# Experts' gate and up products in four column groups of 32 tokens, with the output summed in PSUM

## The chip, the core and the metric

The kernel runs on one core of one Trainium2 chip. The metric is the device time of one execution in microseconds; the time given for a kernel is the median of several runs. One more execution is recorded by the hardware profiler, and every row of a trace below comes from it.

## What is computed

The reference is a model of two blocks on 256 tokens of width 1024, all in float32. The first block has two layers of three mixers (attention, retention, mLSTM), the second one layer of attention and a linear recurrence, and then a mixture of experts. The change touches the experts alone:

```python
logits = (xf @ w_router + b_router).astype(jnp.float32)   # 256 x 32
top_v, top_i = lax.top_k(logits, TOP_K)                   # 4 of 32 experts a token
gates = jax.nn.softmax(top_v, axis=-1)
...
g = xb @ w_gate[e] + b_gate[e]          # 1024 x 1024
u = xb @ w_up[e] + b_up[e]              # 1024 x 1024
g = jnp.minimum(g, SWIGLU_LIMIT)
u = jnp.clip(u, -SWIGLU_LIMIT, SWIGLU_LIMIT)
glu = g * jax.nn.sigmoid(SWIGLU_ALPHA * g)
return ((u + 1.0) * glu) @ w_down[e] + b_down[e]   # 1024 x 1024
```

Each token's four outputs are weighted by its gates and added to x, and a last RMS norm follows. All 32 experts' weights are read, 12 MB an expert. How many tokens an expert gets follows from the reference and its fixed inputs; in order of the experts it is 63, 75, 47, 3, 55, 22, 47, 9, 57, 33, 21, 34, 13, 10, 24, 4, 19, 29, 20, 1, 13, 36, 39, 31, 22, 40, 35, 19, 22, 126, 27, 28. Two have more than 64 (experts 1 and 29), 13 have more than 32.

## The kernel before, in words

Everything runs in one program, written out by hand. The two blocks up to the router take the first 490 us or so. From there on `_build` goes through the 32 experts in a Python loop (L1304), so each expert's instructions stand once in the program.

Weights come in blocks of 128 x 2048 floats (1 MB), four each for gate, up and down, 12 an expert. They lie in slots of SBUF. `give` (L235) puts the next block in the order into a freed slot, on SyncE's queue; `release` (L247) gives a slot back when its last reader is through. SyncE issues strictly in order, so a transfer that waits for its slot holds all later ones. 19 blocks are under way or in place when the loop starts: expert 0's 12 and seven of expert 1.

A token that chose expert e has a rank in e's list. The kernel handles the first 64 ranks in the main path. `pick` (L1177) builds a one-hot of ranks, multiplies it with the normalised tokens (`xg`), copies the result and transposes it into xT, with the gain. `up` (L1228) calls `product` (L1215) for gate and for up: eight blocks of the contraction, each with two matmuls, one for output columns 0 to 511 into PSUM partitions 0 to 63, one for columns 512 to 1023 into partitions 64 to 127. So 64 tokens fill a column group of 64, and two column groups work on the two halves of the output. Every float32 matmul stands as two records in the trace (two passes). A bias matmul with K = 128 (`own`, which picks the expert's rows out of `bias`) is put into the product. `gated` (L1240) is a chain of five steps on VectorE and ScalarE. `down` (L1248) transposes the result, copies it to hT, and runs a third `product`. The output is copied to `ys`. After every second expert `place` (L1197) builds the matrix that brings outputs back to tokens, weighted with the gates, and `add` (L1262) multiplies with it and adds the result to x on VectorE, 8 matmul records for two experts. The down biases are added to x once, at expert 6 (`last_bias`, L1148).

Tokens beyond 64 go through blocks that are run on a condition, on every engine, nested for up to 256 tokens: `more_up` (L1276, its branch is recorded at L1278) repeats pick, gate, up and gating; `more_down` (L1283, recorded at L1284) repeats down, place and add. The eight gate and up slots are released after the first, the four down slots after the second. `foresee` (L1271) issues a hint for TensorE that a branch is likely taken, which means that the block is skipped; for `more_up` it stands after the gate product, for `more_down` after the first eighth of the down product or so.

Of the kernel before, what the change touches and what calls it, by code (L numbers as in the profile page):

```python
# [9 lines left out]
F32 = mybir.dt.float32  # L10
# [7 lines left out]
CAP = 64  # L18
# [8 lines left out]
def _col_layout():  # L27
    at, off = {}, 0
    for name, n in (
        ("norm0", 8), ("norm1", 8), ("y0", 4), ("y1", 4), ("cw0", 16), ("cw1", 16), ("cb0", 4), ("cb1", 4),  # L30
        ("n1g", 8), ("final", 8), ("cw2", 16), ("cb2", 4), ("ba", 8), ("bi", 8), ("lam", 8), ("og", 8), ("n2g", 8),
    ):
        at[name] = (off, n)
        off += n
    return at, off
# [9 lines left out]
def _constants():  # L45
# [38 lines left out]
    add("owner", np.where(p[:, None] // 64 == p[None, :] // 64, p[:, None] % 32, -1))  # L84
# [13 lines left out]
def _prep(i):  # L98
# [27 lines left out]
    b = np.stack([a["b_gate_2"][0], a["b_up_2"][0]], axis=1).reshape(32, 2, 2, 512).transpose(2, 0, 1, 3)  # L126
    z["bias"] = np.stack([b, b], axis=1).reshape(128, 1024)
    z["b_down"] = a["b_down_2"][0][:, :768].reshape(32, 3, 256).transpose(1, 0, 2).reshape(96, 256)
    z["b_down_end"] = a["b_down_2"][0][:, 768:].reshape(32, 2, 128).transpose(1, 0, 2).reshape(64, 128)
# [21 lines left out]
    put("n2g", a["norm2_g_2"][0])  # L151
    z["cols"] = c
# [43 lines left out]
def _build(tc, T, out):  # L196
# [577 lines left out]
    def mixer(xt):  # L774
# [242 lines left out]
        give(13, 15, 16, 17, 18, 21)  # L1017
# [15 lines left out]
        give(4, 5, 6, 7, 11)  # L1033
# [40 lines left out]
    ew = ctx.enter_context(tc.tile_pool(name="ew", bufs=1))  # L1074
    t22, t23 = slot(22), slot(23)
    xh = slot(12).rearrange("p (a b) -> p a b", a=2)
    bias = ew.tile([128, 1024], F32R, name="bias")
    xg, th = t22[:, 0:512], t22[:, 512:1024]
    more_h = [t22[:, 1024:1536], t22[:, 1536:2048], ew.tile([128, 512], F32, name="more")]
    ys, xTs = ([t23[:, o + 512 * k:o + 512 * k + 512] for k in range(2)] for o in (0, 1024))  # L1080
    nc.scalar.dma_start(rbc[0:96, :], T["b_down"])
    gates, rank = (sm(n, 2, 32, bufs=1) for n in ("gates", "rank"))
    count = small.tile([1, 32], I32, name="count", bufs=1)

    t14 = slot(14)

    def split_bias():

        b = t14[:, 256:1280]
        nc.scalar.dma_start(b, T["bias"])  # L1090
        S.activation(bias, b, AF.Copy)
        for p in (slice(32, 64), slice(96, 128)):
            V.tensor_tensor(bias[p], b[p], bias[p].bitcast(F32), op=OP.subtract)

    def router():
        xT = slot(10).rearrange("p (k t) -> p k t", k=8)
        wr, br = t14[:, 0:256], t14[:, 1536:1568]
        lg, mr = (t14[:, o:o + 72].rearrange("p (a b) -> p a b", a=2) for o in (1568, 1640))
        mask, m8, sel, nv = (t14[:, o:o + n].rearrange("p (a b) -> p a b", a=2)
                             for o, n in ((1712, 64), (1776, 16), (1792, 16), (1808, 4)))  # L1100
        nc.scalar.dma_start(wr, T["w_router"])
        load_row(br, "br")
        r, _ = x_stats(1e-5, xh, False, True)
        tt = [bank(n) for n in ("xg", "tr", "st", "y")]
# [10 lines left out]
        t = bank("g")  # L1115
        for hf in range(2):
# [3 lines left out]
            busy(ins, 8 if hf else 4, bank("cb", 2))  # L1120
# [15 lines left out]
        t = bank("u")  # L1136
# [5 lines left out]
        busy(ins, 4, bank("cb", 2))  # L1142
# [4 lines left out]

    def last_bias():  # L1148

        t = bank("tr")  # L1150
        gx = ew.tile([128, 2, 192], F32, name="hotw")[:, :, 0:96]
        V.tensor_copy(gx.rearrange("p a (q e) -> p a q e", q=3), gates[:, :, None, :].to_broadcast([128, 2, 3, 32]))
        for hf in range(2):
            PE.transpose(t[0:96, 128 * hf:128 * hf + 128], gx[:, hf, :], ident)
        V.tensor_copy(one[0:96, :], t[0:96, 0:256])
        for q, w, o in ((0, rbc, 0), (1, rbc, 256), (2, rbc, 512), (0, b_down, 768), (1, b_down, 896)):
            p, n = slice(32 * q, 32 * q + 32), w.shape[-1]
            t = bank("cb", 2)
            for hf in range(2):
                PE.matmul(t[:, n * hf:n * hf + n], one[p, 128 * hf:128 * hf + 128], w[p, :], start=True, stop=True)  # L1160
            d = x[:, :, o:o + n]
            V.tensor_tensor(d, d, two(t[:, 0:2 * n]), op=OP.add)

    router()
    b_down = before[0:64, :]
    nc.scalar.dma_start(b_down, T["b_down_end"])
    four = lambda v: v.rearrange("p (c s t) -> p c s t", c=4, s=2)
    gain = cols[:, COLS["n2g"][0]:COLS["n2g"][0] + 8].rearrange("p (s c) -> p c s", s=2)

    def ranks(e, j):  # L1170
        if not j:
            return rank[:, :, e]
        r = sm("rj", 2)
        V.tensor_scalar(r, rank[:, :, e], -64.0 * j, None, op0=OP.add)
        return r

    def pick(e, j):  # L1177

        r = ranks(e, j)
        one_hot = ew.tile([128, 2, 64], F32, name="hot", bufs=2)  # L1180
        for hf in range(2):
            V.tensor_scalar(one_hot[:, hf, :], slots[:, 0:64], r[:, hf:hf + 1], None, op0=OP.is_equal)  # L1182
# [5 lines left out]
        if e + j == 0:  # L1188
            busy(ins, 2, bank("cb", 2))
# [179 lines left out]
```

## Time and profile before

| what | us |
|---|---|
| median of 3 runs | 1562.95 (1562.74 to 1572.78) |
| the profiled execution | 1557.01 |
| its span, first to last instruction | 1555.1 |
| TensorE busy | 1406.8 |
| VectorE busy | 580.6 |
| ScalarE busy | 306.7 |

Busy time is what an engine's instructions cover, and matmuls that run side by side count once. Terms of the rows: PE is TensorE's matmuls, PEld its weight loads, DVE VectorE, ACT ScalarE, SP SyncE, and a q behind a name is that engine's sequencer, which issues transfers and takes branches. `out<-in` are the program's names (s is a slot; g, u, y, cb, tr, xg and st are PSUM banks), and x with a number is a count.

### The profile page before, as it was taken

Reading aid. Unit: us, or ns where it says so; the run is one execution under the profiler, and the core shown is the slowest. Engines: PE = TensorE matmul, PEld = TensorE weight load, DVE = VectorE, ACT = ScalarE, POOL = GpSimd, SP = SyncE. Lnnn points to the kernel's source line nnn. Section 1 sums busy time; section 2 is a strip of 40 time slices with the busy share of each in tenths; the row PEclk is TensorE's granted clock in tenths of the full one; section 3 lists DMA queues with packets and bytes.
Section 4 is the critical chain, followed back from the end, with each engine's and each line's share of the span. In section 5 each row is a group of like instructions: output and inputs, shape, how many; then the busy total and the mean of one; then the engine's idle time right before and its main releaser. Section 6 shows DMA issues by size and latency. Waiting matters only on the chain. (4 is left out here: it accounts for less than half of the span.)

```text
span 1555.1 us, 17575 instructions
## 1 busy us (share of the span) xinstructions
PE 1406.8 (90%) x6638; PEld 707.5 (45%) x6638; DVE 580.6 (37%) x1238; ACT 306.7 (20%) x551; POOL 170.8 (11%) x100
## 2 busy tenths in 40 slices
PE   7899989999879989999899999998999998999896
PEld 6687877888556333333333333333333333333332
DVE  4856467648786212222122212221222222222123
ACT  4335443454552000000000000000000000000001
POOL 3333333344240000000000000000000000000001
PEclk9899999999889999999999999999999999999998
DMA  8423443444258756999999999999999999999561
GB/s 296 160 91 127 137 163 109 142 148 139 81 196 337 297 210 264 419 417 370 412 401 420 407 416 408 377 419 418 417 418 410 419 419 406 413 420 419 235 252 63
DMA packets 67500, 469.31 MB, mean 302 GB/s; under 512 B 8128, under 2 KB 9440, under 8 KB 11744
## 3 DMA queue, kind: packets, MB, share of 16 engines
q1 hardware_dynamic: 65664, 463.38, 74.4%
q8 instruction: 142, 2.33, 0.6%
q10 hardware_dynamic: 1632, 3.10, 0.6%
q14 instruction: 62, 0.51, 0.1%
HBM read 465.40 MB, written 1.05 MB: 300 GB/s over the span
## 5 line engine op out<-in xcount | busy, mean ns | idle before, releaser
L1223 PE MATMUL g<-s,s 128*64 128x512 f32 x1088 | 289.4, 601 | 25.3 <-PEq L1284 23.4
L1223 PE MATMUL y<-s,hT 128*64 128x512 f32 x1088 | 256.5, 602 | 1.8 <-ACT hT L1253 1.8
L1223 PE MATMUL u<-s,s 128*64 128x512 f32 x1088 | 247.5, 596 | 0.0
L1223 PEld LDWEIGHTS g<-s,s 128*64 128x64 f32 x1088 | 83.3, 136 | 179.1 <-issue 175.2
L1223 PEld LDWEIGHTS y<-s,hT 128*64 128x64 f32 x1088 | 91.5, 139 | 148.4 <-issue 124.7
L355 POOL TENSOR_TENSOR s<-s,s 128x1024 fp32r<-128x1024 f32 (+2 forms) x59 | 135.3, 2296 | 215.6 <-ACT s L352 163.5
L1223 PEld LDWEIGHTS u<-s,s 128*64 128x64 f32 x1088 | 74.6, 137 | 142.7 <-issue 139.3
L1328 DVE COPY s<-y 64x512 f32<-64x512 f32 x32 | 22.0, 689 | 297.4 <-ACTq L1284 280.6
L1343 POOL TENSOR_TENSOR s<-x,s 128x512 f32<-128x512 f32 x4 | 4.9, 1266 | 1081.2 <-DVE x L1269 1081.2
L352 ACT ACTIVATE s<-s 128x1024 fp32r<-128x1024 f32 (+2 forms) x100 | 100.0, 1008 | 115.9 <-PE pja L370 54.5
L369 PE MATMUL pjb<-s,s 128*128 128x512 f32 (+2 forms) x288 | 101.1, 351 | 7.6 <-DVE s L355 7.6
L368 PE MATMUL pjb<-s,s 128*128 128x512 f32 (+2 forms) x288 | 102.0, 354 | 1.1 <-ACT s L399 0.7
L368 PE MATMUL pja<-s,s 128*128 128x512 f32 (+2 forms) x272 | 98.8, 364 | 3.1 <-ACT s L352 2.6
L370 PE MATMUL pjb<-s,s 128*128 128x512 f32 (+2 forms) x288 | 100.3, 348 | 1.2 <-DVE s L355 0.8
L369 PE MATMUL pja<-s,s 128*128 128x512 f32 (+2 forms) x272 | 97.4, 358 | 3.6 <-DVE s L355 3.6
L370 PE MATMUL pja<-s,s 128*128 128x512 f32 (+2 forms) x272 | 96.7, 355 | 0.5 <-DVE s L400 0.5
L1245 DVE TENSOR_SCALAR s<-u 128x512 f32<-128x512 f32 x34 | 23.5, 692 | 178.2 <-PE u L1223 178.2
L355 DVE TENSOR_TENSOR s<-s,s 128x1024 fp32r<-128x1024 f32 (+2 forms) x53 | 69.4, 1312 | 52.7 <-ACT s L352 52.5
L1242 DVE TENSOR_SCALAR gm<-g 128x512 f32<-128x512 f32 x32 | 22.1, 692 | 161.4 <-PE g L1223 161.4
L1186 PE MATMUL xg<-s,hot 128*64 128x512 f32 x272 | 78.4, 599 | 2.5 <-DVE hot L1182 2.5
L1243 ACT ACTIVATE s<-gm 128x512 f32<-128x512 f32 x32 | 20.2, 630 | 303.2 <-DVE gm L1242 303.2
L1269 DVE TENSOR_TENSOR x<-x,cb 128x512 f32<-128x512 f32 x72 | 49.1, 687 | 64.9 <-PE cb L1266 64.8
(357 smaller groups left out, 1509.8 us busy)
## 6 DMA issues: line engine op xcount, KB each, us to landing
s<-in_w_up_dram SPq DMA_DIRECT2D x128, 1024.0 KB, 18.0
s<-in_w_gate_dram SPq DMA_DIRECT2D x128, 1024.0 KB, 18.1
s<-in_w_down_dram SPq DMA_DIRECT2D x128, 1024.0 KB, 12.3
s<-in_w_o_dram SPq DMA_DIRECT2D x12, 1024.0 KB, 4.8
s<-in_w_cqk_dram SPq DMA_DIRECT2D x4, 1024.0 KB, 7.9
s<-in_w_bqk_dram SPq DMA_DIRECT2D x4, 1024.0 KB, 4.9
s<-in_w_bvg_dram SPq DMA_DIRECT2D x4, 1024.0 KB, 5.0
s<-in_w_aq_dram SPq DMA_DIRECT2D x4, 1024.0 KB, 4.8
```

The costliest lines, as they stand in the source:

```text
L352: S.activation(h, w, AF.Copy)
L355: (V if el == "V" else G).tensor_tensor(lo, w, h.bitcast(F32), op=OP.subtract)
L368: PE.matmul(d, ah, bh, start=start, stop=False, skip_group_check=True)
L369: PE.matmul(d, ah, bl, start=False, stop=False, skip_group_check=True)
L370: PE.matmul(d, al, bh, start=False, stop=stop, skip_group_check=True)
L1186: ins = PE.matmul(t[64 * c:64 * c + 64, :], one_hot[:, hf, :], xh[:, hf, 512 * c:512 * c + 512], start=hf == 0, stop=hf == 1)
L1223: ins = PE.matmul(t[o:o + 64, :], a[:, kt % 4, kt // 4, :], w[i][:, 1024 * k + 512 * c:1024 * k + 512 * c + 512], start=kt == 0, stop=kt == 7)
L1242: V.tensor_scalar(gm, tt[0], 7.0, None, op0=OP.min)
L1243: S.activation(th, gm, AF.Tanh, scale=0.851)
L1245: V.tensor_scalar(th, tt[1], 7.0, -7.0, op0=OP.min, op1=OP.max)
L1269: V.tensor_tensor(d, d, t[c], op=OP.add)
L1328: cp(ys[c][p, :], t[p, :])
```

## The change

Tokens are now handled in groups of 32. In `product`, 32 tokens are a column group of 32, and four of these work on the four quarters of 256 output columns, so that a product of 32 tokens has 32 float32 matmuls (64 records) of 256 columns, in place of 16 (32 records) of 512 for 64 tokens. The first 32 ranks always run; ranks 32 to 63 run the same again into the other half of each PSUM bank, inside `tc.If(n > 64 * j + 32)`, and as only matmuls stand in it, only TensorE branches there. Its hint is given the condition itself. The bias is split in two passes of 256 columns.

The gating chain works on both halves at once, so it follows this block. Down runs as four column groups too (two halves of the output, two of the tokens), each matmul still 512 columns. Its result leaves PSUM in two parts (a rounded one on ScalarE, the rest on VectorE), scaled with the tokens' gates. `scatter` multiplies it with the 0/1 matrix that brings it back to tokens, straight into four PSUM banks `total` that hold the sum over all experts; VectorE adds them to x once, at the end. `places` makes that matrix and the gates of the slots from one matmul (a row of ranks and gates, made once by `rank_rows`). `pick` now yields the transposed tokens directly, one half of a pair of experts' picks at each expert, with no copy and no transposes. `last_bias` moves to expert 0 and starts the sums in `total`.

For more than 64 tokens one block `more` replaces the two: pick, places, gate and up (with a half block in it), gating, down and scatter, nested as before. The gate and up slots are released after it. Two slots (10 and 14) that held the router's data are given to weights a little earlier.

```diff
-        give(13, 15, 16, 17, 18, 21)
+        give(13, 14, 15, 16, 17, 18, 21)
...
+    def places(e, j):
+
+        t, m = bank("m2"), "m" if j else ""
+        PE.matmul(t, sel[:, e:e + 1].to_broadcast([64, 128]), rg, start=True, stop=True)
+        back = ew.tile([128, 256], F32R, name="back" + m, bufs=1 if j else 2)
+        g = ew.tile([128, 1], F32, name="g" + m, bufs=2)
+        V.tensor_scalar(back, t[:, 0:256], -64.0 * j, col("slotp", 0), op0=OP.add, op1=OP.is_equal)
+        V.tensor_tensor_reduce(t[:, 256:512], back.bitcast(F32), t[:, 256:512], 1.0, 0.0, OP.mult, OP.add, g)
+        return g, back
+
+    def pick(b, q):
+
+        t = bank("m1").rearrange("p (k n) -> p k n", k=4)
+        for i in range(4):
+            kt = 4 * q + i
             for hf in range(2):
+                PE.matmul(t[:, i, :], xh[:, hf, 128 * kt:128 * kt + 128], hot[:, hf].rearrange("p e s -> p (e s)"), start=hf == 0, stop=hf == 1)
+        V.tensor_tensor(xTs[b % 2][:, 4 * q:4 * q + 4, :], t, gain[:, 4 * q:4 * q + 4, None].to_broadcast([128, 4, 128]), op=OP.mult)
...
-    def product(t, a, w, swap=0, mid=None, at=3):
...
+    def product(t, own, xT, w, m, j):
+
+        d = t[:, 256 * j:256 * j + 256]
+        for kt in range(8):
+            if kt == 6:
+                for k in range(2):
+                    PE.matmul(d, own, bias[:, k, 256 * m:256 * m + 256], start=False, stop=False, skip_group_check=True)
+            for q in range(4):
+                o = 1024 * (kt % 2) + 256 * q
+                last[0] = PE.matmul(d[32 * q:32 * q + 32, :], xT(kt, j), w[4 * m + kt // 2][:, o:o + 256], start=kt == 0, stop=kt == 7,
+                                    skip_group_check=True)
+
+    def up(own, xT, w, n, j, label, between=None):
+
+        tt = [G1, U1]
+        for m in range(2):
+            product(tt[m], own, xT, w, m, 0)
+            if not m:
+                foresee(label, last[0], mybir.EngineType.PE, n > 64 * j + 32)
+            if between and not m:
+                between()
+        with tc.If(n > 64 * j + 32, label=label):
+            for m in range(2):
+                product(tt[m], own, xT, w, m, 1)
         return tt
...
+    def down(a, w, g):
+
+        t = U1
+        for kt in range(8):
+            q, b = divmod(kt, 2)
             for c in range(2):
+                for j in range(2):
+                    o = 64 * c + 32 * j
+                    PE.matmul(t[o:o + 32, :], a[:, j, b, q, :], w[8 + q][:, 1024 * b + 512 * c:1024 * b + 512 * c + 512],
+                              start=kt == 0, stop=kt == 7, skip_group_check=True)
+        yp = yw(F32R)
+        S.activation(yp[0], t, AF.Copy, scale=g)
+        V.scalar_tensor_tensor(yp[1], t, g, yp[0].bitcast(F32), op0=OP.mult, op1=OP.subtract)
+        return yp
+
+    def scatter(back, yp, stop=False):
+
+        for hf in range(2):
+            for k in range(2):
+                for c in range(2):
+                    p = slice(64 * c, 64 * c + 64)
+                    last[0] = PE.matmul(total[hf][c], back[p, 128 * hf:128 * hf + 128], yp[k][p, :], start=False, stop=stop and k == 1,
+                              skip_group_check=True)
...
+    def more(e, own, w, n, np, j):
+
+        with tc.If(n > CAP * j, label=f"more{e}_{j}"):
+            xT, hm = yw(F32)
+            xT = pick_more(e, j, xT)
+            g, back = places(e, j)
+            t = up(own, lambda kt, k: xT[:, kt, 32 * k:32 * k + 32], w, np, j, f"half{e}_{j}")
+            gated(t, hm)
+            scatter(back, down(turned(hm, hTm), w, g))
             if j < 3:
+                more(e, own, w, n, np, j + 1)
...
     for e in range(32):
...
+        t = up(own, lambda kt, k: xT[:, kt, 32 * k:32 * k + 32], w, np, 0, f"half{e}_0", lambda: new.extend(places(e, 0)))
+        g, back = new
+        gated(t, hid, f"more{e}_1")
+        if not e:
             last_bias()
+        if e:
+            scatter(before_it, yp)
+            foresee(f"more{e}_1", last[0], mybir.EngineType.PE)
+        if b < 15:
+            pick(b + 1, i)
+        a = turned(hid, hT)
         n = nc.values_load(count[0:1, e:e + 1], min_val=0, max_val=256)
+        more(e, own, w, n, np, 1)
         for k in range(8):
             release(i0 + k)
+        yp = down(a, w, g)
         for k in range(8, 12):
             release(i0 + k)
```

## Rows read from the trace of the kernel before

**Rows 1.** The page: TensorE's share, transfers in 40 slices, one issue's time to landing.

```profile
PE 1406.8 (90%) x6638; PEld 707.5 (45%) x6638; DVE 580.6 (37%) x1238; ACT 306.7 (20%) x551; POOL 170.8 (11%) x100
...
DMA  8423443444258756999999999999999999999561
GB/s 296 160 91 127 137 163 109 142 148 139 81 196 337 297 210 264 419 417 370 412 401 420 407 416 408 377 419 418 417 418 410 419 419 406 413 420 419 235 252 63
...
s<-in_w_o_dram SPq DMA_DIRECT2D x12, 1024.0 KB, 4.8
```

**Rows 2.** Stages: window and length, busy us by engine, granted clock, transfer share, GB/s.

```profile
500.00:560.00 60.00, 54.72 (x235) 18.86 (x233) 12.89 (x28) 4.87 (x8) 0.00 (x0) 0.97 0.53 213
...
590.00:1421.00 831.00, 768.88 (x3264) 272.63 (x3264) 195.41 (x398) 65.11 (x108) 0.00 (x0) 1.00 0.99 405
1421.00:1483.00 62.00, 55.88 (x250) 20.23 (x250) 13.51 (x32) 4.84 (x8) 0.00 (x0) 1.00 0.69 284
```

**Rows 3.** Timeline of SyncE at experts 1 and 29: start, us, issue.

```profile
528.72 36.61 SPq L243 DMA_DIRECT2D s<-in_w_up_dram  x4
...
1421.70 37.05 SPq L243 DMA_DIRECT2D s<-in_w_up_dram  x4
```

**Rows 4.** Groups by line, 1085 to 1115 us: count, busy us, mean ns, idle before.

```profile
L1223 PE MATMUL u<-s,s 128*64 128x512 f32 x32 | 7.3, 596 | 0.0
L1223 PE MATMUL y<-s,hT 128*64 128x512 f32 x32 | 7.1, 594 | 0.0
...
L1242 DVE TENSOR_SCALAR gm<-g 128x512 f32<-128x512 f32 x1 | 0.7, 692 | 8.1 <-PE g L1223 8.1
...
L1243 ACT ACTIVATE s<-gm 128x512 f32<-128x512 f32 x1 | 0.6, 630 | 9.6 <-DVE gm L1242 9.6
L1251 PE MATMUL tr<-cst,gm 128*128 128x128 f32 x4 | 0.6, 280 | 0.9 <-DVEq L1278 0.9
...
L1253 ACT ACTIVATE hT<-tr 128x512 f32<-128x512 f32 x1 | 0.6, 597 | 5.2 <-PE tr L1251 5.2
...
L1234 PE MATMUL g<-bias,own 128*128 128x512 f32 x1 | 0.5, 502 | 0.0
```

**Rows 5.** Timeline of TensorE: after a bias matmul; one-column weights.

```profile
1121.92 0.65 PE L1223 MATMUL g<-s,s 128*64 128x512 f32 x2
...
490.80 0.28 PE L1141 MATMUL u<-s,one 128*1 128x32 f32 x4
```

**Rows 6.** Small matmuls in the timeline; groups by line in expert 29 and overall.

```profile
486.54 1.87 PE L1118 MATMUL g<-s,s 128*128 128x32 f32 x16
...
L1266 PE MATMUL cb<-s,backm 64*128 64x512 f32 x8 | 3.0, 641 | 0.7 <-DVE x L1269 0.7
...
L1160 PE MATMUL cb<-rbc,one 32*128 32x256 f32 x12 | 3.0, 409 | 0.9 <-DVE one L1155 0.9
```

**Rows 7.** TensorE's branches by line (min/median/max ns), and one hole in the timeline.

```profile
L1284 PEldq COMPARE_BRANCH  x36: 87/1706/6497, 523.3 to 1534.4; - x36
...
L1278 PEldq COMPARE_BRANCH  x36: 74/422/3322, 514.3 to 1526.3; - x36
...
1117.94 1.51 PE L1223 MATMUL g<-s,s 128*64 128x512 f32 x6 [1.82 <-PEq L1284]
```

**Rows 8.** Timeline of TensorE: the first product, the last down product.

```profile
496.23 0.64 PE L1223 MATMUL g<-s,s 128*64 128x512 f32 x1
...
1531.75 7.09 PE L1223 MATMUL y<-s,hT 128*64 128x512 f32 x32 [0.75 <-ACT hT L1253]
```

**Rows 9.** A hole on TensorE near 921 us, and the clock around it.

```profile
921.21 0.63 PE L1251 MATMUL tr<-cst,gm 128*128 128x128 f32 x4 [1.87 <-DVEq L1278]
...
916.00:922.00 6.00, 4.13 (x20) 1.43 (x17) 1.94 (x5) 0.06 (x1) 0.00 (x0) 1.00 0.99 391
922.00:926.00 4.00, 4.00 (x10) 1.41 (x10) 0.00 (x0) 0.54 (x1) 0.00 (x0) 0.57 1.01 416
```

More of the change, by code (lines that the diff above doesn't have):

```diff
@@ L1095, in router, with yw @@
[L1095 to L1100 removed]
+    def yw(dt):
+        t = ew.tile([128, 1024], dt, name="yw")
+        return t[:, 0:512], t[:, 512:1024]
@@ L1156, in last_bias @@
[L1156 to L1182, printed above, removed]
-        t = bank("xg")
+            PE.transpose(t[0:32, 128 * hf:128 * hf + 128], gates[:, hf, :], ident)
@@ L1215, in product @@
-    def product(t, a, w, swap=0, mid=None, at=3):
-        for i in range(4):
-            if i == at and mid:
-                mid()
-            for k in range(2):
-                kt = 2 * i + k
-                for c in range(2):
-                    o = 64 * (c ^ swap)
-                    ins = PE.matmul(t[o:o + 64, :], a[:, kt % 4, kt // 4, :], w[i][:, 1024 * k + 512 * c:1024 * k + 512 * c + 512],
-                              start=kt == 0, stop=kt == 7)
-                    last[0] = ins
-        return ins
@@ L1228, in up @@
-    def up(e, xT, w, label=None):
-        tt, own = [], ew.tile([128, 128], F32R, name="own")
-        V.tensor_scalar(own, owner, float(e), None, op0=OP.is_equal)
-        for m, tag in ((0, "g"), (1, "u")):
-            t = bank(tag)
-            tt.append(t)
-            last[0] = product(t, xT, w[4 * m:4 * m + 4], mid=lambda: PE.matmul(t, own, bias[:, 512 * m:512 * m + 512], start=False, stop=False,
-                                                                     skip_group_check=True))
-            if label and not m:
-                foresee(label, last[0])
-        return tt
@@ L1271, in foresee @@
-    def foresee(label, ins):
-        with tc.issue_after(ins.ins):
-            tc.mark_branch_hint_location(label, hint="LikelyTaken", engines=[mybir.EngineType.PE])
-    def more_up(e, w, n, j):
-        with tc.If(n > CAP * j, label=f"up{e}_{j}"):
-            gated(up(e, pick(e, j), w), xg, more_h[j - 1])
-            if j < 3:
-                more_up(e, w, n, j + 1)
-    def more_down(e, w, n, j):
-        with tc.If(n > CAP * j, label=f"down{e}_{j}"):
-            y = more_h[j - 1]
-            t = down(y, w)
-            busy(last[0], 4, bank("cb", 2))
-            S.activation(y, t, AF.Copy)
-            back = place([(e, j)], "backm")
-            half = lambda c: slice(64 * c, 64 * c + 64)
-            add(lambda c, hf: back[half(c), 128 * hf:128 * hf + 128], lambda c: y[half(c), :])
-            if j < 3:
-                more_down(e, w, n, j + 1)
@@ L1296, in _build @@
-    cur = pick(0, 0)
+        S.activation(d[:, 0], t[:, 0:256], AF.Copy, scale=0.5)
+        V.tensor_scalar(d[:, 1], t[:, 256:512], 0.5, None, op0=OP.mult)
+        return d
+    def down(a, w, g):
+        t = U1
+        for kt in range(8):
+            q, b = divmod(kt, 2)
[8 more added lines that the diff above has]
+        return yp
```

199 lines of the change are left out of this document (97 added, 102 removed).

## The prediction

> **What bounds the kernel now.** The page's two headline parts come first: TensorE is busy 90% of the span, and the transfer engines are full from slice 17 to 37, mostly at 401 to 420 GB/s [rows 1]. So two things stand near their limit, and a busy share alone does not say which one holds the other. The table by stages [rows 2] separates them. From 590 to 1421 us (experts 2 to 28, 27 of them) TensorE is busy 768.9 of 831 us at the full clock, 30.8 us an expert from one to the next, while the transfers run at a share of 0.99. An expert's weights are 12 blocks of 1.049 MB; at 419 GB/s [rows 1] a block takes 2.50 us and an expert 30.0. TensorE is the slower of the two by under a microsecond an expert. Before 590 and after 1421 the transfers are not full (213 to 284 GB/s). SyncE's own queue says why: it hung for 37 us at 528.7 and again at 1421.7 [rows 3], waiting for slots that experts 1 and 29 hold, the two with more than 64 tokens. The kernel is thus: a start, two slow experts, 27 experts on a 30 us floor with TensorE just above it, one very slow expert, two more, a tail.
>
> **Unit costs, before.** The view by lines of one expert [rows 4] gives them. A product is 32 matmul records of 592 to 596 ns in 7.1 us: two column groups run side by side, so a pair advances every 0.44 us. The bias matmul adds 0.5. Vector and ScalarE steps on 128x512 cost 0.63 to 0.69, the four transposes 0.63, the copy to hT 0.60.
>
> **The change, part by part.**
>
> *Gate and up for 32 tokens.* Each product becomes 64 records of 256 columns in four groups. If four run together, 16 steps of half length: 7.1/2 = 3.55 us. If two run together, 32 steps: 7.1. The trace has no 32-column matmul; two rows lie nearest [rows 5]. After the bias two matmuls start at once (two records in 0.65 us, while one alone takes 0.64 [rows 8]), although the code issues both passes of the first group ahead of the second group's, so a group does not queue behind the other. And four one-column load-and-multiply pairs went through in 0.28 us, 0.07 us a pair with the last one's drain in it, so less in a stream; 64 pairs in 3.55 us need 0.055. I take 3.55. Two bias passes of 256 columns cost what one of 512 did, 0.5. H, gate plus up for 32 tokens, is 2 x (3.55 + 0.5) = 8.1 us, against 15.2.
>
> [...]
>
> *Second 32 tokens.* By the counts, 13 of 32 experts have more than 32: H again for them, nothing for 19.
>
> *Picks and places.* A pick issues 16 passes per expert with 128-column loads; 16 such loads with small matmuls took 1.87 us [rows 6]: 1.9, in place of 1.9 for the old pick plus 0.6 for its transposes. `places` adds one matmul between gate and up, like the bias: 0.5, at most twice that.
>
> *Adding to PSUM.* `scatter` is eight 64-row passes of 512 columns. The nearest row is the old extra block's add: eight f32 records in 3.0 us with a wait inside [rows 6]. One pass in place of two and no wait: 1.3, between 0.9 (row halves together) and 1.9 (one after another). The DVE additions into x leave the loop; DVE was idle there, worth nothing.
>
> *The gating chain.* It now begins after the half block: five steps of 0.63 to 0.69 [rows 4] and hand-offs, 4.0 us. Scatter and pick (3.2) run beneath it, so 4.0 stands. Behind the chain's first step VectorE holds the pick's multiplication and half of the copy to hT, which nothing needs sooner. Transposes and copy: 1.2. Down keeps its length, 7.1.
>
> *Branches.* There are two on TensorE per expert before and after. TensorE's compare at the down block took 0.09 to 6.5 us, median 1.7; at the up block median 0.42, where its hint stood far ahead; a typical visible hole was 1.82 [rows 7]. The hints now stand closer: `half` one short product ahead, `more` one pick ahead. Bounds 0.1 and 6.5 each; nearest is the down branch, whose hint also stands a few us ahead, so its median, 1.7 each, 3.4 an expert.
>
> [...]
>
> So an expert costs TensorE 8.1 + 0.5 + 4.0 + 1.2 + 7.1 + 3.4 = 24.3 us with up to 32 tokens and 32.4 with more. An extra block costs pick 3.7 (64-column, twice the loads) + 0.8 + 0.5 + H + 4.0 + 1.2 + 7.1 + 2.6 (out of PSUM, scatter) + 3.4 = 31.4, and 39.5 with a second half. It now holds the eight gate and up slots until its own down is through; before, only the up block did.
>
> **The sum, on the profiled execution (span 1555.1, time 1557.0).**
> - Start: the first product began at 496.2 [rows 8]. Half a pick more and the rank rows ahead of it: 499 (0 to +5).
> - Expert 0: 32.4; `last_bias` stands where scatter would, eight passes of 512 columns by the 12 of 256 in 3.0 us [rows 6], 4.0, with transposes and copy 4.5, and with the pick 6.4 for the chain's 4.0: 2.4 more, 534. Expert 1: 32.4 + 31.4 = 63.8: 598 (before 590), its slots free at 591.
> - Experts 2 to 28: TensorE needs 17 x 24.3 + 10 x 32.4 = 737. The transfers need, for the 317 blocks up to the end of expert 28, 317 x 2.50 = 793, and 2.3 more for the first one (4.8 us to land alone [rows 1]): 1386. The floor decides; rest of down and lag, 1390 (before 1421).
> - Expert 29: its last up block lands 8 blocks later, 1406; then 1.4 (a quarter product and the bias) + 1.7 + 8.1 + 4.0 + 1.2 + 1.7 + 39.5 = 57.6, and down 7.1: 1471 (before 1483).
> - Experts 30 and 31: 24.3 + 22.9 (no pick): 1518. They are TensorE's: the data came during the long block less its empty time.
> - Tail: before, down ended at 1538.8 and the span at 1555.1 [rows 8], 16.3; copies and scatter replace copies and add: 16.3, span 1534.
>
> The profiled run stood 1.9 above its span and 5.9 below the median: 1534 + 8 = 1542 us, 1.3% under 1562.95. TensorE's work falls by far more; the transfer floor and the longer extra blocks eat it.
>
> **Rivals.**
> 1. *The branch waits stay covered* (0.4 each, the up branch's median; an expert 21.7). For: the new hint is given the condition itself. Against: half of the old down branches took 1.7 or more. The floor is met as before; experts 0 and 1: -8, expert 29: -5, the last two: -5, span 1516: 1524.
> 2. *Code for the `more` branch comes late at each expert.* Its compare starts when the transposes are issued; 6.5 less the 1.2 that transposes and copy cover is 5.3, so 27.9 and 36.0 an expert. Above 5.5 us of waits an expert ((793 - 737)/27 + 3.4) the floor no longer hides them. Stages: 608, then 17 x 27.9 + 10 x 36.0 = 834: 1442; expert 29 79, the last two 54, tail 16: span 1591, 1599. [...]
> 3. *Only two groups run together.* Gate and up return to 15.2 per 32 tokens and down doubles to 14.2: 38.5 and 53.7 an expert. By stages: 654 after expert 1, 1192 for the 27, 115, 75 and 16: span 2052, some 2060. For: the trace has no four groups at all. Against: [rows 5].
>
> **How the numbers follow.** Forecast 0.50, its own range 1527 to 1560 (waits of 1 to 2.5 us each); rival 1 0.22, rival 2 0.20, rival 3 0.08. About 1% can be told from no change here, 1547 to 1578. Faster: 0.30 of the forecast and rival 1: 0.52. Same: 0.20 of the forecast, and 0.04 of rival 2: 0.24. Slower: 0.24. The range runs from 1510 (rival 1 with a short start) to 1610 (rival 2), and leaves rival 3 out.
>
> **What would show it.** Four groups: a gate product of 64 records in 3.5 to 3.8 us; 7 is rival 3. The floor: landings of blocks 2.5 us apart and TensorE waiting for DMA in experts 13 to 20, which it hardly does now. Branches: TensorE's compare at `more` at 1.7 us or less in the median (forecast, rival 1), 5 to 6 (rival 2). Transfers must idle near 560 to 590 and near 1435 to 1465. If the middle runs over 31 us an expert, the forecast is wrong.

## The result and the profile after

The changed kernel took 1584.27 us (median of 4 runs, 1581.22 to 1595.89) against 1567.6 of the kernel before on the same chip: ratio 1.0135, 95% interval 1.0092 to 1.0179. It is slower by 1.35%; the forecast was 1.3% faster. (The ratio comes from the fast runs alone and is not the quotient of the two medians, which is 1.011.) Its profiled execution took 1581.22 us with a span of 1578.7, where the forecast had 1534.

The page of the changed kernel (busy time, the clock and the transfers in 40 slices, the queues):

```profile
PE 1308.5 (83%) x12044; PEld 799.3 (51%) x12044; DVE 543.8 (34%) x1157; ACT 282.3 (18%) x517; POOL 171.6 (11%) x100
...
PEclk9899999999889998899899988789899979989877
DMA  7433452344157618999999999999999999999091
...
q8 instruction: 161, 2.64, 0.7%
...
q14 instruction: 50, 0.41, 0.1%
```

Against [rows 1], TensorE's share fell from 90 to 83%, and the transfers are still full in the middle. Around it there are now slices near empty (the 1 ahead of 8 and 9, and the 0 near the end), where the kernel before had dips to 5.

The stages of the changed kernel (window and length, busy us by engine, granted clock, transfer share, GB/s):

```profile
500.00:605.00 105.00, 91.66 (x1041) 49.10 (x1035) 18.97 (x40) 5.10 (x9) 0.00 (x0) 0.92 0.47 191
605.00:1413.00 808.00, 652.26 (x7216) 321.23 (x7214) 156.62 (x312) 44.23 (x78) 0.00 (x0) 0.89 0.99 408
1413.00:1545.00 132.00, 106.40 (x1149) 53.42 (x1149) 22.82 (x45) 6.81 (x12) 0.00 (x0) 0.86 0.69 284
```

The same for the kernel before:

```profile
500.00:605.00 105.00, 96.43 (x418) 33.68 (x414) 21.85 (x46) 7.88 (x13) 0.00 (x0) 0.98 0.61 242
605.00:1413.00 808.00, 747.51 (x3173) 265.62 (x3173) 191.52 (x393) 63.89 (x106) 0.00 (x0) 1.00 0.99 407
1413.00:1545.00 132.00, 118.80 (x516) 42.44 (x512) 31.11 (x65) 11.78 (x22) 2.65 (x3) 1.00 0.59 235
```

In the middle TensorE's work fell by 95 us and bought next to nothing: both kernels move 407 or 408 GB/s there. In the first window the transfers moved less than before (191 GB/s against 242).

SyncE's queue in the changed kernel (start, us, issue) answers to [rows 3]:

```profile
534.40 54.68 SPq L243 DMA_DIRECT2D s<-in_w_up_dram  x4
...
1439.45 58.01 SPq L243 DMA_DIRECT2D s<-in_w_up_dram  x4
```

The queue hangs 55 and 58 us at experts 1 and 29, where it hung 37 before.

TensorE's timeline in expert 19 (start, us, instruction, idle before):

```profile
1118.05 2.78 PE L1236 MATMUL g<-s,s 128*32 128x256 f32 x48
1120.76 0.50 PE L1233 MATMUL g<-bias,own 128*128 128x256 f32 x2
1121.19 1.07 PE L1236 MATMUL g<-s,s 128*32 128x256 f32 x16
...
1127.49 1.07 PE L1236 MATMUL u<-s,s 128*32 128x256 f32 x16 [0.97 <-DMA s<-in_w_up_dram]
...
1132.39 0.66 PE L1269 MATMUL g<-cst,s 128*128 128x128 f32 x4 [0.46 <-DVE s L1259]
1139.16 9.47 PE L1282 MATMUL u<-s,s 128*32 128x512 f32 x64 [6.12 <-PEq L1305]
```

A product of 64 records plus bias takes some 4 us (1118.05 to 1122.2), so four column groups do run together. Then come 6.1 us in which TensorE waits for its own sequencer at `more` (L1305), and a down product of 9.47 us in place of 7.1. The granted clock says why (windows as above):

```profile
1133.00:1139.00 6.00, 0.04 (x1) 0.00 (x0) 0.76 (x4) 0.38 (x1) 0.00 (x0) 0.85 1.00 415
1139.00:1144.00 5.00, 4.84 (x24) 1.35 (x28) 0.22 (x1) 0.00 (x0) 0.00 (x0) 0.50 1.01 418
```

Behind the hole TensorE has 0.50 for the first 5 us of the down product, in which 24 records are counted; in the next 5, at 1.00, it is 56. The transfers beside it run on at 415 to 418 GB/s.

TensorE's compares at `more` (min/median/max ns), which answer to [rows 7]:

```profile
L1305 PEldq COMPARE_BRANCH  x36: 79/3446/6223, 522.8 to 1550.3; - x36
```

One by one, they take 0.4 to 1.5 us in experts 3 to 14 and 5.9 to 6.2 in experts 15 to 28.

### The profile page after: what moved, and what is told of

Same layout as the page of the kernel before. It is cut to its first block, busy times and chain, and to the rows that moved or that the text cites. A ratio compares the mean times of both kernels' runs of the same rounds, so it can differ in the third digit from the quotient of the medians.

```text
span 1578.7 us, 28076 instructions
## 1 busy us (share of the span) xinstructions
PE 1308.5 (83%) x12044; PEld 799.3 (51%) x12044; DVE 543.8 (34%) x1157; ACT 282.3 (18%) x517; POOL 171.6 (11%) x100
## 5 line engine op out<-in xcount | busy, mean ns | idle before, releaser
L1282 PE MATMUL u<-s,s 128*32 128x512 f32 x2176 | 302.1, 710 | 113.2 <-PEq L1305 79.9
L1282 PEld LDWEIGHTS u<-s,s 128*32 128x32 f32 x2176 | 87.1, 128 | 307.4 <-issue 274.4
L1236 PE MATMUL u<-s,s 128*32 128x256 f32 x2880 | 177.7, 382 | 8.6 <-DMA s<-in_w_up_dram 7.0
L1236 PE MATMUL g<-s,s 128*32 128x256 f32 x2880 | 175.7, 381 | 0.0
L1286 DVE SCALAR_TENSOR_TENSOR yw<-u,g,yw 128x512 fp32r<-128x512 f32 x32 | 24.0, 751 | 309.4 <-ACT yw L1285 309.4
L1236 PEld LDWEIGHTS g<-s,s 128*32 128x32 f32 x2880 | 93.5, 110 | 70.3 <-issue 17.1
L1236 PEld LDWEIGHTS u<-s,s 128*32 128x32 f32 x2880 | 83.8, 109 | 74.1 <-issue 11.8
L1285 ACT ACTIVATE yw<-u,g 128x512 fp32r<-128x512 f32 x32 | 22.0, 687 | 392.0 <-PE u L1282 392.0
L1255 DVE TENSOR_SCALAR s<-g 128x512 f32<-128x512 f32 x32 | 22.1, 692 | 174.3 <-PE g L1236 94.6
L1210 PE MATMUL m<-hot,s 128*128 128x128 f32 x512 | 72.7, 299 | 6.7 <-issue 6.1
L1210 PEld LDWEIGHTS m<-hot,s 128*128 128x128 f32 x512 | 66.1, 208 | 18.7 <-issue 17.6
## 6 DMA issues: line engine op xcount, KB each, us to landing
s<-in_w_down_dram SPq DMA_DIRECT2D x128, 1024.0 KB, 15.9
```

Source lines behind the costliest of these rows:

```text
L1210: PE.matmul(t[:, i, :], xh[:, hf, 128 * kt:128 * kt + 128], hot[:, hf].rearrange("p e s -> p (e s)"), start=hf == 0, stop=hf == 1)
L1236: last[0] = PE.matmul(d[32 * q:32 * q + 32, :], xT(kt, j), w[4 * m + kt // 2][:, o:o + 256], start=kt == 0, stop=kt == 7, skip_group_check ...
L1255: V.tensor_scalar(h, tt[0], 7.0, None, op0=OP.min)
L1282: PE.matmul(t[o:o + 32, :], a[:, j, b, q, :], w[8 + q][:, 1024 * b + 512 * c:1024 * b + 512 * c + 512], start=kt == 0, stop=kt == 7, skip_ ...
L1285: S.activation(yp[0], t, AF.Copy, scale=g)
L1286: V.scalar_tensor_tensor(yp[1], t, g, yp[0].bitcast(F32), op0=OP.mult, op1=OP.subtract)
```

## The experiments

Two theories stood at first. **S**: the transfers set the pace in both kernels, and what was lost is their longer idle time at experts 1 and 29, since the merged block holds the slots through its down. **B**: the hole and the low clock at `more` cost the time in every expert. A third, **E**, came out of the first four runs: TensorE sets the pace at both ends, up to expert 2 and from expert 29 on, and the transfers between them. **F** (instruction fetches slow the weights) and **H** (the requests for slots stand behind `more`) were tested on the way.

The runs come from several batches, each beside the kernel before, whose median was 1559 to 1568 us. A difference between two medians of different batches can therefore be off by some 8 us. Ratios to the kernel before compare better; the changed kernel's is 1.0135. The table below, from one trace each, is a third measure.

The table is worked out from the landings of the weight blocks in each trace. The part before the experts varied by up to 15 us between profiled executions (expert 0's first block landed at 434.3 to 449.1 us), so the stretches count from that landing. Fetches are the instruction packets (q8 with 16 KB each, q14 with 8 KB each) in the middle stretch.

| kernel | first block to expert 2's last | to expert 28's last | to the end of the span | fetches |
|---|---|---|---|---|
| before | 144.2 | 817.0 | 157.0 | 99, 38 |
| changed | 168.1 | 808.6 | 165.4 | 108, 28 |
| split, experts 1 and 29 | 157.7 | 820.1 | 167.2 | 108, 28 |
| no `more` in 30 experts | 183.4 | 788.8 | 156.8 | 75, 10 |
| earlier hint | 168.6 | 804.7 | 159.0 | 97, 28 |
| no half block | 154.7 | 797.9 | 142.1 | 94, 28 |
| POOL code | 166.4 | 815.0 | (POOL's) | 108, 71 |
| down first | 183.0 | 950.5 | 176.6 | 121, 28 |
| `more` sooner | 161.1 | 805.3 | 155.1 | 98, 28 |
| `more` sooner, nested hint | 160.1 | 800.2 | 150.5 | 98, 28 |

The changed kernel lost 23.9 us up to expert 2, won 8.4 in the middle and lost 8.4 at the end.

**1. The extra block split in experts 1 and 29.**

```diff
-        more(e, own, w, n, np, 1)
+        if e in (1, 29):
+            more_up(e, own, w, n, np)
+        else:
+            more(e, own, w, n, np, 1)
         for k in range(8):
             release(i0 + k)
+        if e in (1, 29):
+            more_down(e, w, n)
```

`more_up` holds the pick, gate and up, the gating and the transposes; `more_down` holds places, down and scatter.

> Experts 1 and 29 alone: the extra block is cut in two branches. The first picks, multiplies by gate and up, gates and transposes; then the eight gate and up slots are given back; the second multiplies by down and scatters. Theory S (the transfers set the pace in both kernels, and the loss is their longer idle time at experts 1 and 29, 34.2 and 39.6 us against 21.3 and 17.8, because the merged block holds the gate and up slots until its own down is through): the two long landing gaps shrink to about 24 us each and the time falls by 20 to 30 us against the changed kernel, to 1555 to 1565. Theory B (the branch on `more`, with its wait of up to 6.2 us on TensorE in every large expert and the half clock behind it, takes the time): the gaps may shrink but the time stays within 6 us of the changed kernel's 1584.

Measured: 1587.41 us, ratio 1.0204 (1.0156 to 1.0252); no gain; S had expected 20 to 30 us. The slots did come back sooner, and the empty stretches between landings shrank from 34.2 to 25.2 us at expert 1 and from 39.6 to 25.3 at expert 29. But later ones took their place: 21.6 us at expert 3, where it had been 10.5, and a new one of 13.6 at expert 31. So S is too simple: the transfers were let go earlier and then waited for TensorE, which was no earlier (its gate product of expert 2 began at 597.5, in the changed kernel at 598.7).

**2. The `more` branch left out of the program in thirty experts.**

```diff
-        n = nc.values_load(count[0:1, e:e + 1], min_val=0, max_val=256)
-        more(e, own, w, n, np, 1)
+        if e in (1, 29):
+            n = nc.values_load(count[0:1, e:e + 1], min_val=0, max_val=256)
+            more(e, own, w, n, np, 1)
```

> The branch on `more` is in the program for experts 1 and 29 only (the two that take it with this routing); the other thirty have no compare and no code for it. Theory B: the 6 us hole in front of the own down product goes with the clock fall behind it, in 20 or so experts; the time falls by 25 us or more against the changed kernel, below 1560. Theory S: the transfers stay at 30.6 us an expert from expert 2 to 28 and the waits at `more` become waits for DMA; only what the branch adds in experts 1, 29, 30 and 31 can show, at most 4 times 6 = 24 us and more likely under 12: 1572 to 1584.

Measured: 1571.45 us (ratio 1.009, 1.0047 to 1.0132), 13 below the changed kernel by the medians and 7 by the ratios. That is the time S expected, but not for its reason. The middle, which S had standing still, became 20 us shorter, and expert 1 gave 15 us back: TensorE stood 17 us ahead of expert 1's extra block.

```profile
577.09 0.77 PE L1197 MATMUL m<-rg,sel 64*128 64x512 f32 x1 [16.96 <-issue]
```

What TensorE's sequencer did there is in the view of line L1334 (min/median/max ns, first and last start us):

```profile
L1334 PEldq TENSOR_LOAD <-count x32: 297/299/499, 503.3 to 575.9; - x32
```

`values_load` brings an expert's count into its register, one TENSOR_LOAD each, and with the thirty branches gone those of the later experts were moved ahead of the first branch that is left: 26 of them run from 558.4 to 576.6 us, one every 0.7. This is a side effect of the edit. Without it the time would be some 15 us lower, an estimate from the first stretch of the table, and as near to B's as to S's, so the run does not decide between them.

**3. The kernel before, with late releases.**

```diff
-        for k in range(8):
+        for k in range(8 if e not in (1, 29) else 0):
             release(i0 + k)
...
-        for k in range(8, 12):
+        for k in range(8 if e not in (1, 29) else 0, 12):
             release(i0 + k)
```

> The kernel before with one edit: in experts 1 and 29 the eight gate and up slots are given back only after the extra block's down product, as the changed kernel does in effect. Theory S: the idle of the transfers there grows from 21 and 18 us to about 35 to 45 us each and the kernel before gets 25 to 45 us slower, 1592 to 1612. Theory B: the holding costs little, the kernel before stays within 6 us of its 1567.

Measured: 1560.02 us, ratio 1.0006 (0.997 to 1.0042). This is a miss, since the edit did not do what it was to do: the empty stretches stayed 19.3 and 16.8 us, so the run speaks neither for S nor for B. The requests stood later in the program, but waited for the same thing (waits of SyncE in that run: us in total, times, longest):

```profile
SPq L243 <- PEq L1278: 427.4, 31, 31.9
```

What these requests waited for was TensorE at the branch in which the slots' last reader stands (L1278, as in the kernel before: 444.8 us in 31 waits, the longest 33.6), not the place of the request.

**4. An earlier hint for `more`.**

```diff
-            if not m:
+            if j and not m:
                 foresee(label, last[0], mybir.EngineType.PE, n > 64 * j + 32)
+            if early and not m:            # early = f"more{e}_1"
+                foresee(early, last[0], mybir.EngineType.PE)
...
-            foresee(f"more{e}_1", last[0], mybir.EngineType.PE)
```

> The hint for `more` on TensorE is set behind the gate product instead of behind the scatter, and the hint for the half block is left out in the main path, so that the code for `more` is asked for some 10 us ahead of its compare instead of 3 to 4. If the 6.1 us at the compare of `more` is code on its way, it falls below 1 us at most experts. Theory B: the time then falls by 25 us or more, below 1560. Theory S: the time falls by less than 12 us, since the transfers set the pace. The half block's compare may rise from 0.2 to 2 to 6 us in both.

Measured: 1569.54 us (ratio 1.0074, 1.0034 to 1.0113). That is 15 below the changed kernel by the medians, between the two expectations, but 9.5 by the ratios and 9.8 by the table, which S allowed. The compare fell to 0.9 us in the median:

```profile
L1307 PEldq COMPARE_BRANCH  x36: 79/914/6192, 531.7 to 1552.6; - x36
```

And yet the middle became only 3.9 us shorter. B falls: the 6 us holes of the middle were hidden behind the transfers. From 605 to 1413 us TensorE's idle time until weights landed rose from 10 to 40 us, as its holes at `more` shrank from 79 to 45. What was won (6.4 us in the traces) was won at the end, where nothing hides them.

**5. No half block.**

```diff
-            if not m:
+            if j and not m:
                 foresee(label, last[0], mybir.EngineType.PE, n > 64 * j + 32)
...
-        with tc.If(n > 64 * j + 32, label=label):
-            for m in range(2):
-                product(tt[m], own, xT, w, m, 1)
+        if j:
+            with tc.If(n > 64 * j + 32, label=label):
+                for m in range(2):
+                    product(tt[m], own, xT, w, m, 1)
```

> The half block (tokens 33 to 64 of an expert) is left out of the main path with its branch and its hint, so those tokens get no gate and up: TensorE loses 8.1 us in each expert that has more than 32 tokens. Theory E (TensorE sets the pace only at the two ends, from the start to expert 2 and from expert 29 to the end; between them the transfers do): the time falls by about 8 us for each of the experts 0, 1 and 29 that has such tokens, 16 to 26 us, to 1557 to 1567 on the scale of the changed kernel's 1583, and the stretch from expert 2's last block to expert 28's last (808.6 us) changes by less than 20 us. Theory B (TensorE, with its branches, is what the middle waits for): that stretch falls by over 60 us.

Measured: 1541.65 us, ratio 0.9869 (0.9813 to 0.9925), more than expected. The middle, from which some 80 us of TensorE's work went (ten experts), became 10.7 us shorter; the start 13.4 and the end 23.3, of which expert 29's own 8.1 is the part that E had counted. Some 6 us more are TensorE's lag there: expert 29's first up product ended 7.1 us after its last block had landed in the changed kernel, and 1.1 us after it here. The rest was not traced. So the middle is the transfers', the ends are TensorE's.

**6. More instructions, for POOL.**

```diff
+    idle = ew.tile([1, 1], F32, name="idle")
...
+        if 2 < e < 28:
+            for _ in range(384):
+                G.memset(idle, 0.0)
```

> The changed kernel with 384 one-element memsets on the idle POOL in each of the experts 3 to 27; nothing waits for them, they are only more instructions to fetch. Theory F (instructions are fetched over the same DMA engines as the weights, and each fetch costs the weights some time: 102 fetches of 16 KB and a middle of 808.6 us in the changed kernel, 93 and 804.7 with the earlier hint, 72 and 788.8 without the `more` code, so 0.6 us a fetch): some 50 to 80 more fetches of 8 KB, at 0.36 us against 1.07 each, lengthen the middle by 10 to 20 us. Rival: the weights' pace does not depend on the code, and the quicker middle without the `more` code came from TensorE's shorter work: the middle stays within 4 us.

Measured: the middle rose by 6.4 us for 43 more fetches of 8 KB; the rival allowed 4, F wanted at least 10. The run's 1900.34 us says nothing of this, as POOL's own 9600 memsets of 89 ns end 319 us behind TensorE's last matmul.

The table alone overstates F. In the changed kernel's middle three landings, at experts 3, 4 and 5, come 10.5, 5.2 and 4.2 us after the one before; run 2 has no gap over 4 us there. At the usual 2.5 us a block that is 12.4 us of its lead of 19.8, and it is idle time, not code. Between expert 5's last block and expert 27's (264 blocks) the transfers hardly stop, and there the times follow the fetches:

| kernel | 264 blocks, us | fetches of 16 and 8 KB |
|---|---|---|
| no `more` in 30 experts | 667.7 | 63, 9 |
| earlier hint | 671.0 | 83, 24 |
| changed | 673.6 | 92, 24 |
| split (same code there) | 674.4 | 92, 24 |
| POOL code | 680.8 | 92, 62 |

So F holds in direction, and its price of 0.6 us a fetch was too high: 5.9 us for 44 fetches and 7.2 for 38 are 0.13 to 0.19 each, large and small taken alike. That is worked out from one trace each.

**7 and 8. Own down ahead of `more`; and the down bias moved.**

```diff
-        if e:
-            scatter(before_it, yp)
-            foresee(f"more{e}_1", last[0], mybir.EngineType.PE)
         if b < 15:
             pick(b + 1, i)
+            foresee(f"more{e}_1", last[0], mybir.EngineType.PE)
...
+        scatter(back, down(a, w, g), e == 31)
         more(e, own, w, n, np, 1)
-        for k in range(8):
+        for k in range(12):
             release(i0 + k)
-        yp = down(a, w, g)
-        for k in range(8, 12):
-            release(i0 + k)
```

> The own down product and its scatter go ahead of the `more` branch, in the same expert; the hint for `more` is set behind the picks, some 10 us ahead of its compare; all twelve slots are given back behind `more`. [...] Rival H (slots): the gate and up slots come back some 10 us later in each expert, the transfers run dry in more experts and the time rises by 10 us or more.

Measured: 1754.85 us, ratio 1.1271. Theory E had the compare under 1 us in most experts and the time 8 to 15 us lower, at 1568 to 1575; the rival won, by far more than it asked for. SyncE's waits in the changed kernel, and in this one:

```profile
SPq L243 <- PEq L1305: 370.8, 31, 50.2
```

```profile
SPq L243 <- PEq L1305: 692.7, 31, 53.2
```

31 waits on `more` grew from 12 to 22 us each, and the middle grew by 142 us, 5.5 an expert. With the slots given back a down product later, the transfers run dry in every expert (the middle stage of this run: share 0.85, was 0.99):

```profile
605.00:1413.00 808.00, 617.13 (x6030) 309.98 (x6026) 133.87 (x266) 37.41 (x66) 0.00 (x0) 0.84 0.85 345
```

The compare did not fall under 1 us either:

```profile
L1305 PEldq COMPARE_BRANCH  x36: 70/3484/4006, 536.4 to 1736.1; - x36
```

By the records of hint and compare in the trace the hint stood 22 to 25 us ahead here, as the picks it follows ran inside the next gate product. That the distance made the price is not shown: in run 4 a compare with its hint 25.1 us ahead took 0.35 us.

For the eighth run the down bias was moved as well:

```diff
-        if not e:
+        if e == 6:
             last_bias()
```

> As the one above, and the 4.5 us of the down bias in expert 0 moved to expert 6 (there as four products and adds into x, with four clearing products of 64 rows ahead of the first pick in its place). Theory E: TensorE is the bound from the start to expert 1, so expert 1's gate product starts some 3 to 4 us earlier and the end comes 3 to 4 us earlier than in the run above. Rival: the blocks of expert 1 or the gating chain end last there, and nothing is gained (within 1 us by the trace).

Measured: 1753.36 us, 1.5 below its partner, with intervals that largely overlap: no gain can be seen.

**9 and 10. `more` sooner; and the down bias moved.**

```diff
             scatter(before_it, yp)
-            foresee(f"more{e}_1", last[0], mybir.EngineType.PE)
-        if b < 15:
-            pick(b + 1, i)
-        a = turned(hid, hT)
         n = nc.values_load(count[0:1, e:e + 1], min_val=0, max_val=256)
         more(e, own, w, n, np, 1)
         for k in range(8):
             release(i0 + k)
+        if b < 15:
+            pick(b + 1, i)
+        a = turned(hid, hT)
```

> The changed kernel with the hint for `more` behind the gate product (as in the run with the earlier hint) and the `more` branch moved ahead of the picks and the transposes, right behind the scatter: the gating chain of 4 us then runs beside the compare, and the slots come back some 4 to 5 us earlier in each expert. Theory H/E (what counts is when TensorE passes `more`, since the requests for the gate and up slots stand behind it, and how long TensorE takes from expert 29 on): the stretch from expert 29's gate product to the last scatter falls by 5 to 10 us against the 131 of the run with the earlier hint, expert 1 to 3 by some as well, and the time comes 5 to 12 us below that run's 1569, to 1557 to 1564. Rival: the compare still costs its 3 to 6 us and now nothing useful stands behind it, so the time stays within 4 us of 1569.

Measured: 1560.35 us, ratio 0.9993 (0.9953 to 1.0033), 9 below the earlier hint alone by the medians, 13 by the ratios and 10.8 by the table, as H and E had it. The compare costs more again:

```profile
L1307 PEldq COMPARE_BRANCH  x36: 79/3595/5416, 526.8 to 1538.2; - x36
```

So it is not the price of a branch alone that counts, but where it stands: the first stretch is 7.5 and the last 3.9 us shorter than with the earlier hint alone. The gating chain now runs beside the compare, and the slots come back sooner; the run does not separate the two.

> The run above with the 4.5 us of the down bias in expert 0 moved to expert 6. Theory E: TensorE is the bound from the start to expert 1, and 3 to 4 us more are saved against the run above: 1553 to 1561. Rival: nothing is gained.

Measured: 1562.04 us, ratio 0.9979 (0.9948 to 1.0009): no gain over its partner, and the reason can be seen. TensorE's picks of expert 0 in this run, and in the ninth, where the bias stands:

```profile
527.44 3.75 PE L1221 MATMUL m<-hot,s 128*128 128x128 f32 x16 [4.58 <-PEq L1318]
```

```profile
526.34 3.68 PE L1185 MATMUL a<-s,one 32*128 32x512 f32 x8 [0.52 <-DVE one L1182]
530.32 2.02 PE L1210 MATMUL m<-hot,s 128*128 128x128 f32 x16 [0.30 <-PEq L1307]
```

The bias stood where TensorE otherwise waits 4.6 us for its sequencer, which runs seven loads of counts there (522.1 to 526.7 us; three in the ninth run).

**11 and 12. A hint for the nested branch.** In the ninth run the two longest holes on TensorE in experts 1 and 29 were these:

```profile
596.07 3.68 PE L1210 MATMUL m<-hot,s 128*128 128x128 f32 x16 [6.50 <-issue]
...
1491.45 0.45 PE L1271 MATMUL g<-cst,s 128*128 128x128 f32 x1 [3.73 <-DVE own L1335]
```

Both lie behind the extra block's scatter, where `more` asks whether there are more than 128 tokens. That compare had no hint; in the changed kernel, where it had none either, it took 3.9 us in expert 1 and 3.5 in expert 29.

```diff
-            scatter(back, down(turned(hm, hTm), w, g))
+            a = turned(hm, hTm)
+            if j < 3:
+                foresee(f"more{e}_{j + 1}", last[0], mybir.EngineType.PE)
+            scatter(back, down(a, w, g))
```

> The run with `more` moved ahead of the picks, and one more hint: inside `more`, behind its transposes, for the compare of the next level. [...] Theory E: the compare falls under 1 us in both, experts 1 and 29 end 3 to 5 us earlier each, and the time falls by 5 to 9 us against the run without it (1560): 1551 to 1556. [...]

Measured: 1549.33 us, ratio 0.9944 (0.9907 to 0.9981), 11 below the ninth run by the medians, 8 by the ratios and 10.7 by the table: theory E, and somewhat more than it asked. The same two places:

```profile
579.65 2.02 PE L1210 MATMUL m<-hot,s 128*128 128x128 f32 x16 [0.56 <-PEq L1307]
...
1471.30 0.30 PE L1271 MATMUL g<-cst,s 128*128 128x128 f32 x1 [0.56 <-DVE own L1338]
```

The holes are gone. Three small moves (a hint earlier, a branch earlier, a hint added) took the change from 1.0135 to 0.9944 of the kernel before, some 30 us.

> The run above with the down bias of expert 0 moved to expert 6. In the trace of the pair without the nested hint, expert 1's gate product began no earlier by it, once its later start is taken off (the picks stood behind a compare that cost more than the product saved). Within 4 us of the run above.

Measured: 1552.14 us, ratio 0.9937 (0.9911 to 0.9963), as expected the same as its partner. The hint's gain shows in this pair too (0.9979 in run 10, 0.9937 here).

## Why the prediction was wrong

- *Gate and up for 32 tokens*, right: 175.7 us busy in the 2880 records of the gate products is 3.9 for each 64, against 3.55; with its bias the product of expert 19 took 4.2, against 4.05. Four records of four groups start mostly 7 ns apart, at 379 ns a record, so they run side by side. Rival 3 is out.
- *The sum up to expert 1*, right, in part by luck: 598 was forecast for the start of expert 2 and 591 for the slots. TensorE began at 598.7, and SyncE's queue came free at 534.40 + 54.68 = 589.1. But in expert 1 two errors cancel: its four branches left 3.8 us of holes where 6.8 was forecast, and its two downs took 18.5 us in place of 14.2.
- *"The transfers need ... 317 x 2.50 = 793"* is the step that failed most. That the floor decides in the middle was right (runs 4 and 5), its size was not. From the freed queue (589.1) to expert 28's last block (1413.3) those 317 blocks took 824.2 us, 2.60 each. Expert 29's last up block landed at 1434.4 where 1406 was forecast, 28 of the 45 us by which the span missed. Two errors make this up. The 2.50 was the best slice of [rows 1], not the mean; the kernel before's own middle already showed 405 GB/s [rows 2], which is 2.59. Where the transfers hardly stop (run 6), the changed kernel needed 2.55 a block, 16 us more over 317 blocks; part of that is code, as it was 2.53 without `more` in thirty experts. And the sum let the transfers run without a stop from 591 on, while they stood idle for 12.4 us more at experts 3 to 5: TensorE was still behind, and SyncE waited for the branch at `more` (40.3 us in two waits between 595 and 680 us). Ahead of expert 2's compare TensorE's sequencer also runs 12 loads of counts (618.9 to 626.9 us), a term the sum does not have.
- So expert 29 was to start at 1390, 31 us earlier than before, although the sum held the loss ahead of it (slots free at 591, where the queue of [rows 3] came free at 565.3). It started at 1432.7. By the table that loss came in full, 23.9 us up to expert 2, and the middle won back only 8.4. That alone turns the sign.
- *Branches*, 1.7 each: too low at `more`, by over 4 us from expert 15 on, and too high ahead of it. What the price is, the trace shows: 25 of TensorE's 84 compares took over 1.5 us, and in each a 16 KB fetch ends 1.4 to 1.5 us ahead of the compare's end; in none of the 58 under 1 us does a fetch end. Rival 2 had that price right and its place wrong. In the middle it was hidden (run 4: holes down to 0.9 us, middle 3.9 shorter). In experts 29 to 31 it was not: the forecast had 65 us from expert 29's last up block to the end of its own down and 47 for the two after it; measured were 72.6 and 55.8, 16 together. The first part of it: TensorE, held up by the hole of expert 28, ended expert 29's up product 7.1 us after the last up block, where 1.4 was forecast. The rows of the end in the changed kernel:

```profile
1492.68 1.51 PE L1295 MATMUL a<-yw,backm 64*128 64x512 f32 x8 [0.85 <-ACTq L1305]
1497.55 9.47 PE L1282 MATMUL u<-s,s 128*32 128x512 f32 x64 [3.36 <-DVE own L1333]
...
1527.71 9.75 PE L1282 MATMUL u<-s,s 128*32 128x512 f32 x64 [6.57 <-PEq L1305]
...
1554.45 8.34 PE L1282 MATMUL u<-s,s 128*32 128x512 f32 x64 [3.72 <-DVE s L1357]
```

  Holes of 3.4, 6.6 and 3.7 us stand ahead of the three own downs, and the downs take 9.5, 9.8 and 8.3 us in place of 7.1. The releasers named at the first and the last down are short VectorE steps that were over long before; the compare on TensorE ends there. The clock's share was not tried by itself.
- *What would show it*: the test "if the middle runs over 31 us an expert" fired only just (808.6/26 = 31.1). The transfers' idle at expert 1 was where it was said to be (559.9 to 594.1), that at expert 29 came some 30 us later than said (1463.0 to 1502.6). The compare at `more` was to take 1.7 us or less in the median, or 5 to 6 by rival 2; its 3.4 is neither, as the experts fall in two groups. The test that was missing is the length of the idle: the longest gap between landings was 34.2 us at expert 1 and 39.6 at expert 29, 13 and 22 longer than before.
- *Tail*, right: 15.9 us from the last down's end to the end of the span, for 16.3.

## What to carry to other kernels

Ask of a stage what its neighbours hold for it. In the middle of this kernel, where the transfers were the bound (share 0.99), 95 us less work on TensorE made the stage only 8.4 us shorter, and holes of 6 us at `more` were hidden (run 4: 3.9 us); at the ends, where TensorE was the bound, work taken off it was worth 13.4 and 23.3 us (run 5), and a wait at a branch showed in the time (run 11). The gate and up slots came back when TensorE passed the branch that holds their last reader (run 3: 31 waits, 427.4 us in all; run 7: 692.7), so put that branch as early as it can go, with a chain of another engine beside it (run 9: 10.8 us by the table), and give each compare on the rare long path its own hint, here ahead of the extra block's down product (run 11: 10.7 us). Take a floor from the mean pace of the stage (2.60 us a block), not from its best slice (2.50).

## What was not expected of the hardware

- Code competes with weights. A fetch of 16 KB kept one of the 16 DMA engines for 1.07 us in the mean (108 fetches in the changed kernel's middle), and where the transfers hardly stop, blocks came faster with fewer fetches (2.53 us a block with 63 large ones in 264 blocks, 2.55 with 92, and 2.58 with POOL's 38 small ones more).
- What a compare costs goes with when a code fetch ends. In the changed kernel and the kernel before, each of the 47 compares over 1.5 us (25 and 22) ends 1.35 to 1.56 us behind the end of a 16 KB fetch, and in none of the 107 under 1 us does one end. In all traces together 376 compares on TensorE took over 1.5 us, and in every one a 16 KB fetch ended 1.2 to 1.6 us ahead of the compare's end; of 677 under 1 us, 3 had a fetch end inside.
- The hint's distance does not tell the price. In the changed kernel a compare cost 0.4 to 1.5 us with the hint 11 to 19 us ahead and 5.9 to 6.2 with 3 to 5; but run 4 has 5.9 and 6.2 us with the hint 18.6 and 18.5 ahead, and the kernel before has anything from 0.3 to 6.5 with 4.4. In the changed kernel's compares of 5.9 us and more the fetch began only 3.4 to 3.7 us after the compare did. Why it came so late stayed open.
- An engine that seems to wait for nothing can be held by its sequencer, as register loads do not count as busy. A load of a count takes 0.3 us and they come 0.7 us apart; 26 in a row held TensorE for 17 us in run 2. In the kernel before they stand one by one.
